# Gathered rows of a product-key expert layer: their use ranked four gathers later with five places, and twelve prompt products ranked ahead of the last picks

## The chip, the cores and the metric

The kernel runs on one core of one Trainium2 chip. The metric is device time in microseconds of one execution. The engines are named as the profile names them: PE (matrix products), DVE (vector work), ACT (activations and copies), POOL (here it issues the gathers and adds a little), SP (issues the plain loads).

## The reference, cut to what matters

Two layers, each an attention part and then a product-key expert layer. The change lies in the second one. Per token and head the two halves of a query are compared with 128 keys each, the best 16 of each half are combined, and the best 16 of the 256 sums are kept: 128 experts per token, each a row of a table of 16384 rows.

```python
def _peer(h, w_pq, k1, k2, u_tab, v_tab):
    ...
        v1, i1 = lax.top_k(s1, P_TOPK)
        v2, i2 = lax.top_k(s2, P_TOPK)
        cand = (v1[..., :, None] + v2[..., None, :]).reshape(m, P_HEADS, P_TOPK * P_TOPK)
        cid = (i1[..., :, None] * N_KEYS + i2[..., None, :]).reshape(m, P_HEADS, P_TOPK * P_TOPK)
        sc, pick = lax.top_k(cand, P_TOPK)
        eid = jnp.take_along_axis(cid, pick, axis=-1)
        g = jax.nn.softmax(sc, axis=-1)
        u = u_tab[eid]
        a = jax.nn.gelu(jnp.einsum('nhkd,nd->nhk', u, xb).astype(f32), approximate=False)
        coef = (g * a).astype(xb.dtype)
        return jnp.einsum('nhk,nhkd->nd', coef, v_tab[eid])
```

There are 256 prompt tokens (two tiles of 128) and 128 sample tokens (one tile).

## The kernel before, in words

**Two ways to the same sum.** The 256 prompt tokens go through all experts: the tables are streamed once, and a table of gates, zero for experts that a token didn't pick, is multiplied in. The 128 sample tokens fetch only their own rows: expert number s of each of the 128 tokens is one gather of 128 rows of 4 KB, 512 KB in all.

**The picks.** `pick` runs for the sample tile (2) first, then for the prompt tiles 0 and 1: `best` finds the halves' best 16, `scores` the sums, `ids` the kept ones. The last steps of `ids(0)` and `ids(1)` transpose ids and gates on PE into PSUM tiles `pit0` and `pit1` (L760, L761), and DVE casts these into `e_i12` and `e_gp` (L762, L764, L765).

**The prompt's stream.** The 16384 experts are cut into 64 pairs of 128-row blocks. For a pair, `first` loads 1 MB of `peer_u`, forms H with PE, and ACT writes Gelu(H) as `co`. `second` loads 1 MB of `peer_v`, multiplies `co` by the gates `G` on DVE (L943) and adds co · v into four PSUM accumulators `acc`. Most products are made in three passes of split numbers (L159, L160, L161): ACT writes the high part (L153, `u_h`, `v_h`, `ch`), DVE the low one (L156, `u_l`, `v_l`, `cl`). The first 16 pairs' H are plain products (`plain_first`, 32 matmuls each, L881; eviction with Gelu to `e_co`, L883) of `hf`, a sum that POOL makes (L869). In `ahead` ten of them, H0 to H9, are emitted behind the whole of `pick`; the other six between the builds. All go through one PSUM pool, `po_`, which has one bank; `at` is a pool of three.

**The gates.** A gate table for 16 blocks is built in 16 steps of 16 tokens: one-hot rows As (DVE L905, or ACT L900), B (DVE L909, L912), their product on PE (`gp`, L920), and an ACT copy to `G`. The 16 builds of tables 0 and 1 stand ahead of `second(0)`; those of the tables 2 to 7 are spread over pairs 8 to 47. As0 of the first 16 builds takes one of the two places of the `peer_v` loads until these builds are through.

**The sample's rows.** `gather_slots` emits gathers behind each pair by `SLOTS`: three per pair up to pair 16, then 4 1/3. The first 128 rows are of `peer_u`: DVE takes the dot product of each with the token's vector (L850). Then come a Gelu and 128 rows of `peer_v`, which DVE adds to `x_s` (L853). There are `ROWB` = 4 places for rows; a gather (POOL, L845) waits until its place is free. Gather and use are emitted together.

**What sets the order.** A list scheduler takes the order in which instructions are emitted as their rank, and puts them on each engine by its own idea of when they are ready. On the chip each engine then works through its list in order: whatever stands first in it holds up all behind it. SP issues the loads of `peer_u` and `peer_v` in its own order, two places for each.

Of the kernel before, what the change touches and what calls it, by code (L numbers as in the profile page):

```python
# [10 lines left out]
F16 = mybir.dt.float16  # L11
# [3 lines left out]
AF = mybir.ActivationFunctionType  # L15
ALU = mybir.AluOpType
# [9 lines left out]
B = 8  # L26
# [15 lines left out]
TB = 16  # L42


PLAIN = (3, 6, 9, 11, 13, 15)
AHEAD = (10, 16)
BUILDS = (((2, 3), 8, 16), ((4, 5), 16, 32), ((6, 7), 32, 48))
SLOTS = ((0, 0), (16, 48), (64, 256))

# [3 lines left out]

RAW = 2
RAWV = 2
ROWB = 4


ORDER = mybir.DependencyInfo(mybir.DependencyClass.NoSync, mybir.DependencyReason.SCHED_ONLY)
# [17 lines left out]
def tile_stream_encoder(ctx: ExitStack, tc: tile.TileContext, I, O, stop=None):  # L77
    nc = tc.nc
    V, S, G, PE = nc.vector, nc.scalar, nc.gpsimd, nc.tensor
# [13 lines left out]
    def po_(name):  # L93
        return pso.tile([128, 512], F32, name=name, tag="po")
# [530 lines left out]
        return out  # L625


    def pick(l, hT, hS, kp, dst, after):

        L = f"l{l}p"  # L630
        qT = kp.tile([128, 8, T], F32, name=L + "_qT", bufs=1)
# [146 lines left out]
        ids(2)  # L778
        best(1, 0)
        best(1, 1)  # L780
        scores(1)
        ids(0)
        ids(1)
# [8 lines left out]
    def peer(l, rest):  # L792
        L = f"l{l}e"
        with tc.tile_pool(name=L, bufs=1, reuse_waits="tile") as lp:

            rings = [lp.tile([128, 4096], F32, name=f"{L}_co{i}", tag="ring", bufs=2) for i in range(2)]
            hT = [lp.tile([128, KC, TP], F32R, name=f"{L}_h{i}") for i in range(2)]
            xn_s = lp.tile([128, D], F32, name=L + "_xn")
            dst = {
                "g": lp.tile([128, 8, 16], F32, name=L + "_g"),  # L800
                "eid": lp.tile([128, 128], I32, name=L + "_eid"),
                "ni1": lp.tile([128, TP], F32, name=L + "_ni1"),
                "i12": lp.tile([128, 2, TP], F16, name=L + "_i12"),
                "gp": lp.tile([128, 2, TP], F16, name=L + "_gp"),
            }
            ex = Experts(l, hT, xn_s, dst, lp, rings)
            with tc.tile_pool(name=L + "k", bufs=2, reuse_waits="tile") as kp:
                def big(name, *shape):
                    return carve(kp.tile([128, 1024], F32, name=name, tag="big", bufs=3), shape)

                hS = [kp.tile([128, KC, 128], F32R, name=f"{L}_hs{i}", tag="dl", bufs=4) for i in range(2)]
                done = norm(I["norm2"][l], lambda t: hS if t == 2 else [h[:, :, t * 128:t * 128 + 128] for h in hT],
                     big, kp, L + "_n2", (2, 0, 1), xn_s, rest)
                pick(l, hT, hS, kp, dst, done[0])
                if stop == (l, "pick"):
                    return
                ex.ahead()
            with tc.tile_pool(name=L + "g", bufs=2, reuse_waits="tile") as gp:
                ex.run(gp)

    class Experts:
        def __init__(self, l, hT, xn_s, dst, lp, rings):
            self.l, self.L, self.hT, self.xn_s, self.dst, self.lp = l, f"l{l}x", hT, xn_s, dst, lp
            self.act = lp.tile([128, 128], F32, name=self.L + "_act")
            self.tables = [I[n].rearrange("l e d -> (l e) d") for n in ("peer_u", "peer_v")]
            self.places = [carve(r, (8, 512)) for r in rings]
            self.co, self.G, self.slot = {}, {}, 0

        def load(self, n, pb):

# [8 lines left out]
        def gather_slots(self, n):  # L839

            for _ in range(min(n, 256 - self.slot)):
                which, s = divmod(self.slot, 128)
                self.slot += 1
                row = self.lp.tile([128, D], F32, name=f"{self.L}_row{which}_{s}", tag="row", bufs=ROWB)
                G.indirect_dma_start(out=row, out_offset=None, in_=self.tables[which],  # L845
                                     in_offset=bass.IndirectOffsetOnAxis(ap=self.dst["eid"][:, s:s + 1], axis=0),
                                     element_offset=self.l * NE * D)
                act = self.act
                if which == 0:
                    V.scalar_tensor_tensor(row, row, 1.0, self.xn_s, op0=ALU.mult, op1=ALU.mult,  # L850
                                           accum_out=act[:, s:s + 1])
                else:
                    V.scalar_tensor_tensor(x[2], row, act[:, s:s + 1], x[2], op0=ALU.mult, op1=ALU.add)  # L853
                if self.slot == 128:
                    S.activation(act, act, AF.Gelu)
                    V.tensor_tensor(act, act, self.dst["g"].rearrange("p h k -> p (h k)"), ALU.mult)

        def ahead(self):

# [13 lines left out]
        def plain_first(self, pbs):  # L873

            L, hf = self.L, self.hf
            for pb in pbs:
                ps = po_(f"{L}_H{pb}")
                u = carve(self.load("u", pb), (2, KC, 128))
                for i in range(2):
                    for k in range(KC):  # L880
# [4 lines left out]
        def build(self, es, tb):  # L885
# [17 lines left out]
            else:  # L903
# [1 line left out]
                V.tensor_tensor(A, iota_2[:, None].to_broadcast([128, NP, 128, 2]), pairs(dst["i12"][:, 0], 128),  # L905
                                ALU.is_equal)
                first = [A[:, t // 2, :, t % 2] for t in range(TB)]
            Bt = carve(self.gp.tile([128, 2 * 48 * TB], F16, name=f"{L}_B{es[0]}{tb}", tag="B"), (2, NP, n, 2))
            V.tensor_tensor(Bt[:, 1], iota_2[:, None, es[0] * 16:es[0] * 16 + n, :].to_broadcast([128, NP, n, 2]),  # L909
                            pairs(dst["i12"][:, 1], n), ALU.is_equal)  # L910
            for i in range(2):
# [177 lines left out]
```

## Time and profile before

| | |
|---|---|
| median of 3 runs | 2651.66 us (2648.11 to 2671.17) |
| profiled execution | 2656.09 us, span 2654.3 us |
| layer 0, layer 1 | about 0 to 1330, 1330 to 2654 us |
| PE busy | 2465.4 us, 93% |
| DVE busy | 2157.9 us, 81% |
| ACT busy | 1416.3 us, 53% |
| POOL busy | 891.0 us, 34% |
| HBM read | 631.48 MB, 240 GB/s over the span |
| mean granted clock of PE | 0.970 |

The busy shares are averages over stages of different kind. In layer 0 the picks end and the first builds begin at about 530 us, the first product of `second` starts at 601.55 us, the last gate build is done at about 1158 us, the last row is used at about 1290 us and the stream ends at about 1328 us; layer 1 repeats this some 1325 us later.

### The profile page before, as it was taken

What the parts mean: (1) busy time and instruction counts of PE and PEld (TensorE: products, weight loads), DVE (VectorE), ACT (ScalarE), POOL (GpSimd) and SP (SyncE); (2) the same over time, 40 slices, a digit from 0 to 9 for tenths busy, and PEclk for the clock granted to TensorE, in tenths of its full rate; (3) what the DMA queues carried; (4) which work ended last, traced back from release to release, by engine and by line L of the source; (5) the groups of instructions that cost most, each with busy time, mean ns of one, the idle gap of its engine ahead of it and who ended that gap; (6) DMA issues with size and microseconds to landing.
All of it is one profiled execution on the core that took longest, in us unless ns stands there. A gap on an engine that the chain in (4) does not pass through costs nothing.

```text
span 2654.3 us, 45318 instructions
## 1 busy us (share of the span) xinstructions
PE 2465.4 (93%) x17316; PEld 2073.8 (78%) x17316; DVE 2157.9 (81%) x4346; ACT 1416.3 (53%) x2594; POOL 891.0 (34%) x587
## 2 busy tenths in 40 slices
PE   7889998898999999999989999988989999999999
PEld 6757777686688888888877677777766888888887
DVE  5754468998999999998767554699989999999986
ACT  4344334273787787744443442332637786876443
POOL 1100010144444565666210000101444455656661
PEclk9999999899999999999999998998999999999999
DMA  4242531498889899999632344314988999999995
GB/s 173 88 128 85 163 120 55 152 352 309 306 321 338 328 340 327 338 345 351 239 112 92 124 132 131 111 57 162 346 316 302 332 334 333 338 329 333 358 349 198
DMA packets 172011, 640.15 MB, mean 241 GB/s; under 512 B 20880, under 2 KB 37008, under 8 KB 139024
## 3 DMA queue, kind: packets, MB, share of 16 engines
q1 hardware_dynamic: 98064, 368.77, 39.0%
q0 software_dynamic: 73728, 268.47, 27.8%
q8 instruction: 136, 2.23, 0.3%
q14 instruction: 83, 0.68, 0.1%
HBM read 631.48 MB, written 5.70 MB: 240 GB/s over the span
## 4 chain that ended last, share of the span: by engine, by line
PE 31%; issue 23%; DVE 18%; POOL 15%; DMA 11%; ACT 2%; POOLq 0%; SPq 0%; DVEq 0%; ACTq 0%
POOL l0x_row L845 8%; POOL l1x_row L845 7%; DMA l0x_row<-in_peer_v_dram,l0e_eid 6%; DMA l1x_row<-in_peer_v_dram,l1e_eid 4%; DVE x_s L853 1%; PE l_g_ps L159 1%; PE l_g_ps L160 1%; PE l_g_ps L161 1%; PE l_pa_ps L159 1%; PE l_pa_ps L160 1%; PE l_pa_ps L161 1%; PE l1x_acc L161 1%; PE l1x_acc L160 1%; PE l1x_acc L159 1%; PE l_br_ps L161 1%
## 5 line engine op out<-in xcount | busy, mean ns | idle before, releaser
L845 POOL DMA_INDIRECT l0x_row<-in_peer_v_dram,l0e_eid x128 | 237.9, 1858 | 152.8 <-DVE x_s L853 135.2
L845 POOL DMA_INDIRECT l1x_row<-in_peer_v_dram,l1e_eid x128 | 238.5, 1863 | 149.4 <-DVE x_s L853 127.1
L845 POOL DMA_INDIRECT l1x_row<-in_peer_u_dram,l1e_eid x128 | 172.0, 1344 | 266.6 <-DVE l1x_row L850 229.7
L845 POOL DMA_INDIRECT l0x_row<-in_peer_u_dram,l0e_eid x128 | 171.1, 1336 | 268.7 <-DVE l0x_row L850 231.0
L161 PE MATMUL l0x_H<-l0e_h,l0x_u_l 128*128 128x256 f32 x768 | 219.7, 286 | 3.6 <-DVE l0x_u_l L156 3.6
L161 PE MATMUL l1x_H<-l1e_h,l1x_u_l 128*128 128x256 f32 x768 | 218.8, 285 | 3.4 <-DVE l1x_u_l L156 3.4
L159 PE MATMUL l0x_H<-l0e_h,l0x_u_h 128*128 128x256 f32 x768 | 221.9, 289 | 0.0
L159 PE MATMUL l1x_H<-l1e_h,l1x_u_h 128*128 128x256 f32 x768 | 221.0, 288 | 0.0
L160 PE MATMUL l0x_H<-l0e_h,l0x_u_h 128*128 128x256 f32 x768 | 219.2, 285 | 0.0
L160 PE MATMUL l1x_H<-l1e_h,l1x_u_h 128*128 128x256 f32 x768 | 218.2, 284 | 0.0
L160 PE MATMUL l0x_acc<-l0x_v_l,l0x_ch 128*128 128x512 f32 x464 | 186.3, 402 | 13.2 <-DVE l0x_v_l L156 13.2
L160 PE MATMUL l1x_acc<-l1x_v_l,l1x_ch 128*128 128x512 f32 x464 | 185.4, 400 | 13.9 <-DVE l1x_v_l L156 13.8
L159 PE MATMUL l0x_acc<-l0x_v_h,l0x_ch 128*128 128x512 f32 x464 | 186.2, 401 | 8.3 <-ACT l0x_v_h L153 4.3
L159 PE MATMUL l1x_acc<-l1x_v_h,l1x_ch 128*128 128x512 f32 x464 | 185.1, 399 | 7.5 <-ACT l1x_ch L153 4.5
L853 DVE SCALAR_TENSOR_TENSOR x_s<-l0x_row,l0x_act,x_s 128x1024 f32<-128x1024 f32 x128 | 166.0, 1297 | 25.1 <-DMA l0x_row<-in_peer_v_dram,l0e_eid 24.4
L161 PE MATMUL l0x_acc<-l0x_v_h,l0x_cl 128*128 128x512 f32 x464 | 183.8, 396 | 0.0
L161 PE MATMUL l1x_acc<-l1x_v_h,l1x_cl 128*128 128x512 f32 x464 | 183.0, 394 | 0.7 <-DVE l1x_cl L156 0.7
L853 DVE SCALAR_TENSOR_TENSOR x_s<-l1x_row,l1x_act,x_s 128x1024 f32<-128x1024 f32 x128 | 164.2, 1282 | 23.8 <-DMA l1x_row<-in_peer_v_dram,l1e_eid 23.0
L850 DVE SCALAR_TENSOR_TENSOR l0x_row<-l0x_row,l0e_xn 128x1024 f32<-128x1024 f32 x128 | 155.9, 1227 | 32.4 <-DMA l0x_row<-in_peer_u_dram,l0e_eid 31.9
L850 DVE SCALAR_TENSOR_TENSOR l1x_row<-l1x_row,l1e_xn 128x1024 f32<-128x1024 f32 x128 | 155.5, 1225 | 31.0 <-DMA l1x_row<-in_peer_u_dram,l1e_eid 30.9
L153 ACT ACTIVATE l0x_v_h<-l0x_v 128x1024 fp32r<-128x1024 f32 x116 | 121.3, 1051 | 98.4 <-DMA l0x_v<-in_peer_vt_dram 51.2
L153 ACT ACTIVATE l1x_v_h<-l1x_v 128x1024 fp32r<-128x1024 f32 x116 | 121.4, 1051 | 96.6 <-DMA l1x_v<-in_peer_vt_dram 47.2
(530 smaller groups left out, 7334.4 us busy)
## 6 DMA issues: line engine op xcount, KB each, us to landing
l0x_u_raw<-in_peer_ut_dram SPq DMA_DIRECT2D x64, 1024.0 KB, 7.1
l0x_v<-in_peer_vt_dram SPq DMA_DIRECT2D x64, 1024.0 KB, 7.5
l1x_u_raw<-in_peer_ut_dram SPq DMA_DIRECT2D x64, 1024.0 KB, 7.3
l1x_v<-in_peer_vt_dram SPq DMA_DIRECT2D x64, 1024.0 KB, 7.6
l_g_raw<-in_w_in_dram SPq DMA_DIRECT2D x16, 1024.0 KB, 4.9
l_pa_raw<-in_w_in_dram SPq DMA_DIRECT2D x8, 1024.0 KB, 5.0
l_kbT<-in_cache_b_kT_dram SPq DMA_DIRECT2D x16, 512.0 KB, 4.0
l_cvb<-in_cache_b_vt_dram SPq DMA_DIRECT2D x16, 512.0 KB, 4.6
```

Source lines behind the costliest of these rows:

```text
L153: op = S.activation(hi, src, AF.Copy)
L159: PE.matmul(out, lh, rh, start=start, stop=False)
L160: PE.matmul(out, lh, rl, start=False, stop=False)
L161: PE.matmul(out, ll, rh, start=False, stop=stop)
L845: G.indirect_dma_start(out=row, out_offset=None, in_=self.tables[which], in_offset=bass.IndirectOffsetOnAxis(ap=self.dst["eid"][:, s:s + 1 ...
L850: V.scalar_tensor_tensor(row, row, 1.0, self.xn_s, op0=ALU.mult, op1=ALU.mult, accum_out=act[:, s:s + 1])
L853: V.scalar_tensor_tensor(x[2], row, act[:, s:s + 1], x[2], op0=ALU.mult, op1=ALU.add)
```

## The change

It has four parts. `ROWB` goes from 4 to 5. The use of a row is emitted when four more gathers have been emitted (`ROWLAG` = 4, `use_row`), so that its rank is that much lower; the last ones are flushed with the 256th gather. `ahead` is handed to `pick` as `meanwhile` and emitted between `best(1, 1)` and `scores(1)`, `ids(0)`, `ids(1)`, with twelve plain products in place of ten, and the plain products go in turn to `po_` and `at`. The tile for B is cut from 48 to 32 columns per token, which are all that a build uses, and frees the room for the fifth row. Lines behind the edits are shifted by one to seven: L850 is L857, L853 L855, L881 L885, L905 L909, L920 L924.

```diff
-AHEAD = (10, 16)
+AHEAD = (12, 16)
...
-ROWB = 4
+ROWB = 5
+ROWLAG = 4
...
         best(1, 1)
+        meanwhile()
         scores(1)
         ids(0)
         ids(1)
...
-                pick(l, hT, hS, kp, dst, done[0])
-                if stop == (l, "pick"):
-                    return
-                ex.ahead()
+                pick(l, hT, hS, kp, dst, done[0], ex.ahead)
...
-                act = self.act
-                if which == 0:
-                    V.scalar_tensor_tensor(row, row, 1.0, self.xn_s, op0=ALU.mult, op1=ALU.mult,
-                                           accum_out=act[:, s:s + 1])
-                else:
-                    V.scalar_tensor_tensor(x[2], row, act[:, s:s + 1], x[2], op0=ALU.mult, op1=ALU.add)
-                if self.slot == 128:
-                    S.activation(act, act, AF.Gelu)
-                    V.tensor_tensor(act, act, self.dst["g"].rearrange("p h k -> p (h k)"), ALU.mult)
+                self.rows.append((which, s, row))
+                while len(self.rows) > (ROWLAG if self.slot < 256 else 0):
+                    self.use_row(*self.rows.pop(0))
+
+        def use_row(self, which, s, row):
+
+            act = self.act
+            if which == 1:
+                V.scalar_tensor_tensor(x[2], row, act[:, s:s + 1], x[2], op0=ALU.mult, op1=ALU.add)
+                return
+            V.scalar_tensor_tensor(row, row, 1.0, self.xn_s, op0=ALU.mult, op1=ALU.mult, accum_out=act[:, s:s + 1])
+            if s == 127:
+                S.activation(act, act, AF.Gelu)
+                V.tensor_tensor(act, act, self.dst["g"].rearrange("p h k -> p (h k)"), ALU.mult)
...
-                ps = po_(f"{L}_H{pb}")
+                ps = (po_, at)[pb % 2](f"{L}_H{pb}")
...
-            Bt = carve(self.gp.tile([128, 2 * 48 * TB], F16, name=f"{L}_B{es[0]}{tb}", tag="B"), (2, NP, n, 2))
+            Bt = carve(self.gp.tile([128, 2 * 32 * TB], F16, name=f"{L}_B{es[0]}{tb}", tag="B"), (2, NP, n, 2))
```

The lists of POOL are the same before and after; on SP the loads of `v0` and `v1` stand one or two `peer_u` loads later. The lists of DVE and PE differ in both layers alike. On DVE of layer 0, where the picks end, the list before was this (`row_2` is a use of gathered row 2, `p_e` a last step of the picks, `e_i` and `e_gp` the casts out of `pit`):

```order
L850 SCALAR_TENSOR_TENSOR l0x_row_2_5233,l0x_act<-l0x_row_2_5233,l0e_xn 128x1024
L735 TENSOR_TENSOR l0p_e_4115<-l0p_we_4110 128x128
L850 SCALAR_TENSOR_TENSOR l0x_row_3_5275,l0x_act<-l0x_row_3_5275,l0e_xn 128x1024
L762 CAST l0e_i_3051<-l0p_pit_4121 128x2x128
L905 TENSOR_TENSOR l0x_As_4344<-iota_91,l0e_i_3051 128x2048
L764 CAST l0e_gp<-l0p_pit_4121 128x128
L909 TENSOR_TENSOR l0x_B_4346<-iota_91,l0e_i_3051 128x512
```

and after it is this:

```order
L857 SCALAR_TENSOR_TENSOR l0x_row_3_5272,l0x_act<-l0x_row_3_5272,l0e_xn 128x1024
L736 TENSOR_TENSOR l0p_e_4366<-l0p_we_4361 128x128
L857 SCALAR_TENSOR_TENSOR l0x_row_4_5274,l0x_act<-l0x_row_4_5274,l0e_xn 128x1024
...
L857 SCALAR_TENSOR_TENSOR l0x_row_14_5393,l0x_act<-l0x_row_14_5393,l0e_xn 128x1024
L763 CAST l0e_i_3051<-l0p_pit_4334 128x2x128
L763 CAST l0e_i_3051<-l0p_pit_4372 128x2x128
L765 CAST l0e_gp<-l0p_pit_4334 128x128
L909 TENSOR_TENSOR l0x_As_4384<-iota_91,l0e_i_3051 128x2048
```

The line of "..." stands for rows 5 to 13, one behind the other. Before, four row uses stood ahead of the first one-hot rows; after, fifteen do, and the casts that the builds begin with stand behind them.

On PE of layer 0, in the same place, the list before was this (H6 to H8 are plain products, `pit` the transposes that the casts read, `gp00` the first build):

```order
L881 MATMUL l0x_H6_4260<-l0x_hf_4137,l0x_u6_raw_4261 128x256 x8
L761 MATMUL l0p_pit0_4083<-cst_70,l0p_g0_3841 128x128
L881 MATMUL l0x_H7_4280<-l0x_hf_4137,l0x_u7_raw_4281 128x256 x12
...
L881 MATMUL l0x_H8_4300<-l0x_hf_4137,l0x_u8_raw_4301 128x256 x7
...
L761 MATMUL l0p_pit1_4121<-cst_70,l0p_g1_4046 128x128
L881 MATMUL l0x_H8_4300<-l0x_hf_4137,l0x_u8_raw_4301 128x256 x9
...
L920 MATMUL l0x_gp00_4352<-l0x_B00_4346,l0x_As0_4344 128x32
```

and after it is this:

```order
L885 MATMUL l0x_H6_4116<-l0x_hf_3993,l0x_u6_raw_4117 128x256 x16
...
L885 MATMUL l0x_H11_4216<-l0x_hf_3993,l0x_u11_raw_4217 128x256 x16
L761 MATMUL l0p_pit0_4334<-cst_70,l0p_fi0_4330 128x128 x2
L762 MATMUL l0p_pit0_4334<-cst_70,l0p_g0_3841 128x128
L761 MATMUL l0p_pit1_4372<-cst_70,l0p_fi1_4368 128x128 x2
L762 MATMUL l0p_pit1_4372<-cst_70,l0p_g1_4297 128x128
L885 MATMUL l0x_H12_4563<-l0x_hf_3993,l0x_u12_raw_4564 128x256 x8
...
L924 MATMUL l0x_gp00_4392<-l0x_B00_4386,l0x_As0_4384 128x32
```

H6 to H11 now stand in one piece ahead of the transposes of both tiles, and four products, H12 to H15, are left for the stretch of the builds, where seven were.

Farther on the row uses stand 9 to 12 rows further in DVE's list than they did. At the split of `v` of pair 20 it was this before (`row0_93` is the 94th row of `peer_u`):

```order
L850 SCALAR_TENSOR_TENSOR l0x_row0_91_8431,l0x_act_3053<-l0x_row0_91_8431,l0e_xn_3047 128x1024
L850 SCALAR_TENSOR_TENSOR l0x_row0_92_8434,l0x_act_3053<-l0x_row0_92_8434,l0e_xn_3047 128x1024
L850 SCALAR_TENSOR_TENSOR l0x_row0_93_8437,l0x_act_3053<-l0x_row0_93_8437,l0e_xn_3047 128x1024
L156 TENSOR_TENSOR l0x_v200_l_7362<-l0x_v20_7359,l0x_v200_h_7361 128x1024
L156 TENSOR_TENSOR l0x_v201_l_7378<-l0x_v20_7359,l0x_v201_h_7377 128x1024
```

and after:

```order
L857 SCALAR_TENSOR_TENSOR l0x_row0_102_8756,l0x_act_3053<-l0x_row0_102_8756,l0e_xn_3047 128x1024
L857 SCALAR_TENSOR_TENSOR l0x_row0_103_8759,l0x_act_3053<-l0x_row0_103_8759,l0e_xn_3047 128x1024
L857 SCALAR_TENSOR_TENSOR l0x_row0_104_8918,l0x_act_3053<-l0x_row0_104_8918,l0e_xn_3047 128x1024
L157 TENSOR_TENSOR l0x_v200_l_7358<-l0x_v20_7355,l0x_v200_h_7357 128x1024
L157 TENSOR_TENSOR l0x_v201_l_7374<-l0x_v20_7355,l0x_v201_h_7373 128x1024
```

So the uses, emitted four gathers later, are placed earlier against the stream: row 104 instead of row 93 stands just ahead of this split. Ahead of the first `cl` (pair 0) it is row 37 instead of 28.

## Rows read from the trace of the kernel before

**Rows 1.** Windows of layer 0 (start:end, length, busy per engine, clock, DMA share, GB/s).

```profile
530.00:601.00 71.00, 66.67 (x749) 57.91 (x748) 66.87 (x123) 50.98 (x128) 32.12 (x26) 1.00 0.94 355
601.00:753.00 152.00, 136.79 (x1005) 99.27 (x1004) 130.09 (x210) 79.77 (x171) 66.07 (x49) 0.93 0.84 307
753.00:1140.00 387.00, 380.47 (x3229) 342.06 (x3228) 370.23 (x462) 298.46 (x575) 215.57 (x124) 1.00 0.91 333
1140.00:1300.00 160.00, 150.54 (x944) 133.56 (x943) 144.28 (x134) 66.40 (x79) 91.44 (x53) 0.97 0.93 342
1300.00:1328.00 28.00, 28.00 (x156) 24.49 (x155) 14.85 (x14) 12.83 (x16) 0.96 (x1) 1.00 0.35 119
```

**Rows 2.** Waits of PE and DVE, 601 to 1328 us (us in total, times, longest).

```profile
PE l0x_acc L160 <- DVE l0x_v_l L156: 13.2, 12, 4.3
PE l0x_gp L920 <- DVE l0x_B L912: 6.0, 6, 1.8
PE l0x_acc L159 <- ACT l0x_v_h L153: 4.3, 1, 4.3
PE l0x_acc L159 <- ACT l0x_ch L153: 4.0, 1, 4.0
PE l0x_H L161 <- DVE l0x_u_l L156: 3.6, 5, 1.9
DVE l0x_row L850 <- DMA l0x_row<-in_peer_u_dram,l0e_eid: 28.3, 21, 5.7
DVE x_s L853 <- DMA l0x_row<-in_peer_v_dram,l0e_eid: 24.4, 23, 2.5
```

**Rows 3.** Timeline of POOL: gathers 4, 5 and 7 (start, us; idle time before).

```profile
524.88 0.94 POOL L845 DMA_INDIRECT l0x_row<-in_peer_u_dram,l0e_eid  x1 [42.13 <-DVE l0x_row L850]
526.41 1.88 POOL L845 DMA_INDIRECT l0x_row<-in_peer_u_dram,l0e_eid  x1 [0.60 <-DVE l0p_we L733]
529.88 1.99 POOL L845 DMA_INDIRECT l0x_row<-in_peer_u_dram,l0e_eid  x1 [0.31 <-issue]
```

**Rows 4.** Timeline of DVE where picks end (start, us; idle time before it).

```profile
523.37 1.23 DVE L850 SCALAR_TENSOR_TENSOR l0x_row<-l0x_row,l0e_xn 128x1024 f32<-128x1024 f32 x1
529.50 0.42 DVE L762 CAST l0e_i<-l0p_pit 128x256 f16<-128x256 f32 x1 [0.73 <-PE l0p_pit L761]
535.11 1.23 DVE L850 SCALAR_TENSOR_TENSOR l0x_row<-l0x_row,l0e_xn 128x1024 f32<-128x1024 f32 x1 [0.33 <-DMA l0x_row<-in_peer_u_dram,l0e_eid]
540.04 1.23 DVE L850 SCALAR_TENSOR_TENSOR l0x_row<-l0x_row,l0e_xn 128x1024 f32<-128x1024 f32 x1 [2.42 <-DMA l0x_row<-in_peer_u_dram,l0e_eid]
```

**Rows 5.** Timeline of PE around the plain products.

```profile
449.04 1.99 PE L881 MATMUL l0x_H<-l0x_hf,l0x_u_raw 128*128 128x256 f32 x8 [2.58 <-POOL l0x_hf L869]
495.71 7.17 PE L881 MATMUL l0x_H<-l0x_hf,l0x_u_raw 128*128 128x256 f32 x32 [0.69 <-ACT l0e_co L883]
507.58 6.16 PE L881 MATMUL l0x_H<-l0x_hf,l0x_u_raw 128*128 128x256 f32 x16 [4.69 <-ACT l0e_co L883]
```

**Rows 6.** DVE from 529.5 to 601.5 us, by form (busy, mean ns, idle before).

```profile
L850 DVE SCALAR_TENSOR_TENSOR l0x_row<-l0x_row,l0e_xn 128x1024 f32<-128x1024 f32 x25 | 30.8, 1231 | 3.8 <-DMA l0x_row<-in_peer_u_dram,l0e_eid 3.6
```

**Rows 7.** Timeline of PE: half-speed products behind two waits.

```profile
658.52 0.79 PE L160 MATMUL l0x_acc<-l0x_v_l,l0x_ch 128*128 128x512 f32 x1 [4.35 <-DVE l0x_v_l L156]
659.11 0.63 PE L161 MATMUL l0x_acc<-l0x_v_h,l0x_cl 128*128 128x512 f32 x1
663.54 0.39 PE L161 MATMUL l0x_acc<-l0x_v_h,l0x_cl 128*128 128x512 f32 x1
```

**Rows 8.** Timeline of DVE and ACT before that: the row and the loads awaited.

```profile
656.09 1.23 DVE L850 SCALAR_TENSOR_TENSOR l0x_row<-l0x_row,l0e_xn 128x1024 f32<-128x1024 f32 x1 [5.66 <-DMA l0x_row<-in_peer_u_dram,l0e_eid]
652.27 2.00 ACT L153 ACTIVATE l0x_v_h<-l0x_v 128x1024 fp32r<-128x1024 f32 x2 [10.34 <-DMA l0x_v<-in_peer_vt_dram]
```

**Rows 9.** Waits of PE, 420 to 601 us.

```profile
PE l0x_H L881 <- ACT l0e_co L883: 13.9, 9, 4.7
```

**Rows 10.** Waits of DVE in layer 1, 1927 to 2648 us.

```profile
DVE l1x_row L850 <- DMA l1x_row<-in_peer_u_dram,l1e_eid: 25.8, 20, 4.8
```

More of the change, by code (lines that the diff above doesn't have):

```diff
@@ L625, in transpose_s, with pick @@
         return out
-    def pick(l, hT, hS, kp, dst, after):
+    def pick(l, hT, hS, kp, dst, after, meanwhile):
         L = f"l{l}p"
@@ L826, in __init__ @@
             self.places = [carve(r, (8, 512)) for r in rings]
-            self.co, self.G, self.slot = {}, {}, 0
+            self.co, self.G, self.slot, self.rows = {}, {}, 0, []
         def load(self, n, pb):
```

## The prediction

> **What bounds the kernel now.** I read the windows by stage first, since the change touches two of them. The reader is to see there which engine has the least slack. In the stretch of the first builds, 530 to 601 us, DVE is busy 66.87 of 71 us, PE 66.67, and the DMA engines run at 0.94 [rows 1]. In the stream behind it PE is the bound: 136.79 of 152 us, 380.47 of 387, 150.54 of 160, 28.00 of 28. So from the start of `second` to its end (727 us) PE has only 15.2 + 6.5 + 9.5 = 31 us without work, and half of that lies in the first 152 us. Then I read who ends PE's waits: 13.2 us for DVE's `v_l`, 6.0 for B, 4.3 and 4.0 for ACT, 3.6 for `u_l`, 31.1 in all [rows 2]. DVE in the same time waits 28.3 + 24.4 = 52.7 us for gathered rows [rows 2]. A split that stands behind an awaited row in DVE's list is late by that wait; the clearest place is 656 us, where DVE waits 5.66 us for a row and PE then 4.35 us for `v_l` [rows 7, 8]. Layer 1 shows the same (25.8 us for its `peer_u` rows) [rows 10], so I work out one layer and double it.
>
> **The change part by part.**
>
> *Row uses ahead of the casts.* This part of the order is what I hold to be decisive at the start of the builds. Before, row uses 0 to 3 stand ahead of the cast, their rows were fetched during the picks, and the casts are done at 529.5 us [rows 4]. Now uses 0 to 14 stand ahead of it. Five gathers can be in flight; the fifth goes out during the picks, as the others do. Gather 5 needs the place of row 0, whose use is over about when it is now, so it goes out at some 524 us, where gather 4 goes out before [rows 3]; gathers 6 to 9 follow each of the next uses by 531 us. From issue to use it took 526.41 to 535.11 us (8.7) and 529.88 to 540.04 (10.2) [rows 3, 4]. Gather 10 goes out when row 5 is used (about 534), gather 14 when row 9 is used. Two rounds of 8.7 us behind the use of row 4 at about 532 us and the last uses end at 532 + 17.4 + 1.2 = 551 us; with 10.2 it is 554, and if the last rows share the DMA engines with plain loads that PE takes one each 7.17 us, 556. The quickest two rounds that I allow, 7.6 us, give 549. The uses themselves, 11 by 1.23 us, are work that is taken from later. PE gets to the transposes at 449.0 + 12 x 7.17 = 535 us at the earliest [rows 5], perhaps 540, so the rows end last. The casts come 21.5 us later than at 529.5 (19.5 to 27).
>
> *The stretch of the builds.* From the cast to the first `cl` DVE had 71.1 us, with 25 row uses and 3.8 us of waits for rows [rows 6]. It now has 23 row uses and none of those waits, but both casts: 71.1 - 3.8 - 2 x 1.3 + 1 = 66 us. PE has four plain products there instead of seven, so DVE stays the bound. A row each 2.9 us, with five in flight and about 9 to 11 us from use to use, leaves the rows in time. `second` starts at 551 + 66 = 617 to 618 us instead of 601.5: **17 us lost** (14 to 22).
>
> *Plain products earlier, in two pools.* PE's waits for the eviction of `e_co`, 13.9 us and up to 4.69 us each, go [rows 5, 9]. They lie where DVE works without pause on the picks, and the builds wait for DVE: nothing is won. If the cover were gone, these 13.9 us would be the price; of a cost of the second pool I see no row; a product that waits there for a bank would do so in the same cover.
>
> *Five places and later use in the stream.* A place goes round in: use, POOL's issue of 0.94 to 1.99 us, 8 to 10 us of transfer, the next use. That is about 11 us. Behind 601 us some 227 rows are used until about 1290, one each 3.0 us on the mean, and rather 2.85 us where there are 4 1/3 per pair instead of three: four places give 11.4 us, just at the edge, which is why DVE waits often and little (24.4 us in 23 waits [rows 2]); five give 14.2 us. So most of the 52.7 us of DVE's waits go. What PE gets of it is bounded: from below by 0 (its waits then come from the `v` loads: at 652.27 us ACT had waited 10.34 us for one [rows 8]), from above by its idle time less what rows don't cause. From 601 to 753 us DVE itself has 130 us of work, and the DMA share of 0.84 would be 0.95 at 134 us, so at most 18 us, with the half-speed products behind the waits included (0.43 instead of 0.23 us from start to start [rows 7]). From 753 to 1140 at most 6.5; from 1140 to 1300 at most 9, without the 4.0 us for `ch`, which is the last build's. Behind it row uses stand about 11 rows further in the list; these 11 x 1.3 us of DVE work and 5.5 MB of transfers were done while it waited for the casts. At the end, where PE is busy 28.00 of 28 us, some 3 us may come from a tail that isn't held by rows. Together **0 to 37 us; I take 25**, two thirds, because the rows are named as what holds the splits, and since PE is at 98% in the longest stretch already.
>
> *B's smaller tile, the SP order.* The same instructions on the same elements: 0. `v0` and `v1` behind one or two more `u` loads are needed only at 617 us: 0.
>
> Sum per layer: +17 - 25 = -8 us, twice -16. The profiled execution took 2656.09 us, so 2640; the median of the runs lies 4.4 us below that execution. **2636 us** as a median.
>
> **The rivals.**
>
> *All row waits go.* The gain is the bound of 37 us, the lost start 17 to 18: -19 per layer, 2651.7 - 38 = **2614**. For it: five places against a cycle just at four's edge. Against it: PE's other sources of waits, and DMA at 0.91 to 0.93.
>
> *The lost start isn't won back (slower).* The mechanism: until As0 gives its place back, `v` loads have one place; then the stream's first 50 us hang on `v` loads, for one of which ACT waited 10.34 us [rows 8]. With five rows in flight these loads share the DMA engines with one gather more, so the `v_h` splits get later, not earlier, and the row waits only change into waits for `v`. With 17 us lost and 0 to 3 won, it is +15 per layer: 2651.7 + 31 = **2683**. It decides when the stream's gain is under some 4 us per layer. Against it: the rows use 11 gathers less of the transfers behind 601 us.
>
> *Only the transposes count.* If the rows land during PE's products, as would be with 4 us per round, the casts run at 540 us: some 6 us are lost after the row uses done early, 25 won, 2651.7 - 38 = **2614** again. Against it are all transfers of [rows 3, 4].
>
> *A slow clock in the builds.* PE would have no work for some 16 us between the transposes and the first build. Behind 4.3 us of waiting twice, products started 0.43 us apart instead of 0.23, until 662.5 us [rows 7]. If PE ran at the low level (1.2 GHz) for the whole stretch of builds, its four plain products (4 x 7.17 = 29 us) and its builds (66.67 us less 7.3 plain products, about 14 us [rows 1, 5]) would take up to twice 43 us, well over DVE's 66, though some of it would lie in PE's pauses: some 7 to 10 us per layer on top, which leaves **2654**. For it: builds are short, and DVE feeds PE piecemeal. Against it: in the builds of before, of the same kind, the granted clock was 1.00 [rows 1]. The Trainium skill, "TensorE: Matmul & The Clock Gate", section "What's actually happening", says that throttled is the default state and that activity releases it, which speaks for this rival; the row at full clock shows release with plain products among the builds, and no row here shows what four instead of seven of them do.
>
> *A rule weighed.* Gathers took POOL 0.94 us at 524.88 and 1.88 and 1.99 us at 526.41 and 529.88, where DVE was at work on picks and tables [rows 3]. The Trainium skill, "SBUF — State Buffer", section "Who interferes with whom", says that POOL's making of descriptors can be shut out by DVE's two-port operations; the trace fits that. While DVE only waits for rows 5 to 14 each gather would then take 0.94 us, and the builds would start 2 us earlier than 551 us. By the rows alone it is 551, which I keep.
>
> **How the numbers follow.** Chances: forecast 0.42 (own range 2618 to 2655, from a gain of 17 to 33 and a start of 14 to 22), all row waits go 0.22, slower 0.20, slow clock 0.08, transposes only 0.08. About 1% (26.5 us) is what a measurement of this kernel can tell: under 2625 is faster, over 2678 slower. Of the forecast a fifth lies under 2625, of the second and the last case most: 0.08 + 0.20 + 0.07 = 0.35. Of the slower case most lies over 2678, with a little of the clock: 0.17. The rest, 0.48, is within 1%. The range leaves out the best tail of the second case and the worst of the third: 2600 to 2688.
>
> **What would show it.** In the profile after: DVE waits for DMA at rows 5 to 14 ahead of the casts, some 15 us, and the first build at 551 us; PE's waits for `e_co` gone; first product of `second` at 617 us; DVE's row waits behind it under 15 us per layer; the 152 us behind the start down to some 137; PE's waits for `v_l` down from 13.2 to under 4 us. The prediction fails if row waits persist at five places (then transfers get longer, not rarer), if `v` loads take the waits over, or if the casts come near 540 us.

## The result and the profile after

Over 15 runs of each, the median went from 2661.06 to 2641.51 us; the ratio is 0.9935 with the interval 0.9919 to 0.9952, some 17 us. The two profiled executions differ by 12.2 us (2656.09 and 2643.86). The page's first lines for the changed kernel:

```profile
span 2642.1 us, 45319 instructions
PE 2447.8 (93%) x17316; PEld 2072.3 (78%) x17316; DVE 2157.1 (82%) x4346; ACT 1421.1 (54%) x2594; POOL 902.9 (34%) x587
```

The instructions are the same to a handful; PE is busy 17.6 us less. First to where the picks end, in DVE's timeline of layer 0 after (start, duration, and in brackets the idle time before and what ended it):

```profile
528.58 1.21 DVE L857 SCALAR_TENSOR_TENSOR l0x_row<-l0x_row,l0e_xn 128x1024 f32<-128x1024 f32 x1
538.48 1.23 DVE L857 SCALAR_TENSOR_TENSOR l0x_row<-l0x_row,l0e_xn 128x1024 f32<-128x1024 f32 x1 [6.00 <-DMA l0x_row<-in_peer_u_dram,l0e_eid]
546.44 1.23 DVE L857 SCALAR_TENSOR_TENSOR l0x_row<-l0x_row,l0e_xn 128x1024 f32<-128x1024 f32 x1 [2.55 <-DMA l0x_row<-in_peer_u_dram,l0e_eid]
552.48 1.22 DVE L857 SCALAR_TENSOR_TENSOR l0x_row<-l0x_row,l0e_xn 128x1024 f32<-128x1024 f32 x1
553.63 0.75 DVE L763 CAST l0e_i<-l0p_pit 128x256 f16<-128x256 f32 x2
```

Against [rows 4] the casts are 24.1 us late. The first line is the use of row 4, the last use is that of row 14, and between them DVE waits 11.4 us in all for gathers (6.00, 2.55 and three shorter waits). PE's timeline over the same stretch and the builds:

```profile
508.40 27.89 PE L885 MATMUL l0x_H<-l0x_hf,l0x_u_raw 128*128 128x256 f32 x128 [0.30 <-ACT l0e_co L887]
536.68 0.27 PE L762 MATMUL l0p_pit<-cst,l0p_g 128*128 128x128 f32 x1
557.13 0.21 PE L924 MATMUL l0x_gp<-l0x_B,l0x_As 128*128 128x32 f16 x1 [14.68 <-DVE l0x_B L916]
623.35 7.63 PE L885 MATMUL l0x_H<-l0x_hf,l0x_u_raw 128*128 128x256 f32 x28
630.64 0.58 PE L160 MATMUL l0x_acc<-l0x_v_h,l0x_ch 128*128 128x512 f32 x1
```

The four products in 27.89 us have no wait for `e_co` left among them, where [rows 9] had 13.9 us. The transposes are done at 537 us; then PE waits for DVE. The first product of `second` comes at 630.64 us instead of 601.55, and in layer 1 at 1945.37 instead of 1927.36, which is 27.6 us later counted from the layer's first norm. PE's and DVE's waits in the builds, 553.6 to 627 us (us in total, times, longest):

```profile
PE l0x_gp L924 <- DVE l0x_B L916: 21.5, 7, 14.7
PE l0x_gp L924 <- ACT l0x_As L904: 17.9, 3, 7.9
DVE l0x_B L913 <- PE l0x_gp L924: 4.1, 2, 2.4
DVE l0x_As L909 <- PE l0x_gp L924: 2.8, 5, 1.3
```

Of the 21.5 us 14.7 are the wait shown above, most of which lies ahead of the casts. In the kernel before, from 529.5 to 600.6 us, PE waited 3.3 us for B and not for As:

```profile
PE l0x_gp L920 <- DVE l0x_B L912: 3.3, 4, 2.1
```

Now it waits for ACT's As too, and DVE waits 6.9 us for PE's gate products. Then the stream. Windows cut at the same work tell more than windows at the same time: from the first product of `second` to the eviction of H16, to that of H31, to that of H63. First the kernel before (start:end, length, busy time of PE, PEld, DVE, ACT, POOL with instructions, PE clock, DMA share, GB/s):

```profile
601.55:719.57 118.02, 105.88 (x739) 74.21 (x738) 101.32 (x164) 62.49 (x136) 49.09 (x38) 0.94 0.84 305
719.57:915.99 196.42, 189.84 (x1614) 168.01 (x1613) 184.46 (x271) 150.04 (x297) 90.14 (x65) 0.97 0.90 330
915.99:1314.23 398.24, 385.75 (x2914) 345.30 (x2913) 365.70 (x378) 238.53 (x402) 234.68 (x125) 0.99 0.91 333
```

and the changed kernel:

```profile
630.64:742.68 112.04, 105.42 (x740) 73.87 (x739) 102.07 (x164) 62.39 (x137) 55.35 (x40) 0.97 0.85 320
742.68:927.43 184.75, 184.75 (x1613) 164.65 (x1613) 182.15 (x259) 150.47 (x296) 100.97 (x65) 1.00 0.94 349
927.43:1304.36 376.93, 376.62 (x2914) 341.91 (x2913) 352.63 (x367) 240.86 (x401) 214.73 (x112) 1.00 0.89 335
```

The stream takes 673.7 us instead of 712.7. The reader should see that two things went: in the two long windows PE's idle time (19.1 us, now 0.3), and 14.2 us of its busy time for the same matmuls, with the clock at 1.00 in place of 0.97 and 0.99. The low level (0.50) accounts for a part of these 14.2 us only. In the two windows of the kernel before it was granted in these four stretches:

```profile
741.23:748.06 6.83, 6.02 (x79) 5.94 (x76) 6.83 (x13) 3.93 (x13) 3.35 (x3) 0.50 0.73 283
901.66:905.07 3.41, 3.41 (x9) 2.65 (x8) 3.34 (x6) 3.41 (x9) 0.45 (x1) 0.50 0.86 312
1154.25:1161.07 6.82, 6.32 (x14) 4.64 (x15) 6.82 (x9) 4.03 (x6) 2.93 (x2) 0.50 0.91 311
1236.17:1239.58 3.41, 3.41 (x18) 3.41 (x17) 3.41 (x4) 1.60 (x3) 1.90 (x2) 0.50 0.86 296
```

PE was busy for 19.2 us of them; at twice the clock that work would take no less than half of that, so the clock makes at most 9.6 us (an estimate from these rows). Where the other 4.6 us come from wasn't taken apart. The waits behind the start, 627 to 1322 us:

```profile
PE l0x_acc L160 <- ACT l0x_v_h L154: 3.0, 1, 3.0
PE l0x_gp L924 <- DVE l0x_B L916: 2.8, 5, 0.9
PE l0x_acc L161 <- DVE l0x_v_l L157: 0.7, 1, 0.7
DVE l0x_row L857 <- DMA l0x_row<-in_peer_u_dram,l0e_eid: 10.0, 11, 2.4
DVE x_s L855 <- DMA l0x_row<-in_peer_v_dram,l0e_eid: 1.7, 4, 0.8
```

They answer to [rows 2]: DVE's 52.7 us for rows are 11.7, PE's 13.2 for `v_l` are 0.7. Layer 0 of the profiled execution gains 39.0 us in the stream and loses 29.1 at its start; the next layer's first transposes start at 1326.48 instead of 1336.10 us. Layer 1 gains less, and the rest of this text reads layer 0 unless it says otherwise: its stream, from the first product of `second` to the eviction of H63, takes 676.28 us instead of 706.52, so 30.2 us are won against the 27.6 lost at the start. First before, then after:

```profile
1927.36:2633.88 706.52, 676.88 (x5263) 583.94 (x5262) 649.37 (x811) 451.34 (x831) 370.70 (x223) 0.99 0.89 328
1945.37:2621.65 676.28, 667.41 (x5263) 580.53 (x5262) 635.43 (x789) 454.27 (x831) 364.57 (x213) 0.99 0.90 333
```

The two layers' balances, 9.9 and 2.6 us, are the 12.2 us of the profiled executions but for 0.3.

### The profile page after: what moved, and what is told of

Read it like the earlier page. It is cut to its first block, busy times and chain, and to the rows that moved or that the text cites. A ratio compares the mean times of both kernels' runs of the same rounds, so it can differ in the third digit from the quotient of the medians.

```text
span 2642.1 us, 45319 instructions
## 1 busy us (share of the span) xinstructions
PE 2447.8 (93%) x17316; PEld 2072.3 (78%) x17316; DVE 2157.1 (82%) x4346; ACT 1421.1 (54%) x2594; POOL 902.9 (34%) x587
## 4 chain that ended last, share of the span: by engine, by line
PE 67%; DVE 17%; issue 8%; POOL 3%; DMA 3%; ACT 2%; SPq 0%; POOLq 0%; ACTq 0%; DVEq 0%
PE l0x_H L160 4%; PE l1x_H L160 4%; PE l0x_H L162 3%; PE l1x_H L162 3%; PE l1x_H L161 3%; PE l0x_H L161 3%; PE l1x_acc L160 3%; PE l1x_acc L161 3%; PE l0x_acc L162 3%; PE l0x_acc L160 3%; PE l1x_acc L162 3%; PE l0x_acc L161 3%; POOL l0x_row L844 2%; POOL l1x_row L844 2%; PE l_g_ps L160 1%
## 5 line engine op out<-in xcount | busy, mean ns | idle before, releaser
L857 DVE SCALAR_TENSOR_TENSOR l1x_row<-l1x_row,l1e_xn 128x1024 f32<-128x1024 f32 x128 | 154.3, 1221 | 25.5 <-DMA l1x_row<-in_peer_u_dram,l1e_eid 25.1
L857 DVE SCALAR_TENSOR_TENSOR l0x_row<-l0x_row,l0e_xn 128x1024 f32<-128x1024 f32 x128 | 154.8, 1223 | 21.9 <-DMA l0x_row<-in_peer_u_dram,l0e_eid 21.5
L855 DVE SCALAR_TENSOR_TENSOR x_s<-l0x_row,l0x_act,x_s 128x1024 f32<-128x1024 f32 x128 | 165.4, 1292 | 3.7 <-DMA l0x_row<-in_peer_v_dram,l0e_eid 1.7
L855 DVE SCALAR_TENSOR_TENSOR x_s<-l1x_row,l1x_act,x_s 128x1024 f32<-128x1024 f32 x128 | 163.6, 1278 | 3.4 <-DMA l1x_row<-in_peer_v_dram,l1e_eid 2.6
```

## The experiments

Two theories: A, the fifth place gains and the new order costs; B, the eleven row uses done while DVE waits for the tables are the gain. All ratios are against the kernel before. In the table are, for layer 0 in us, the last cast of the ids (`e_i`), the start of `second`, the stretch between (builds) and from the start to the eviction of H63 (stream).

| run | casts | start | builds | stream | ratio (95%) |
|---|---|---|---|---|---|
| before | 529.5 | 601.6 | 72.1 | 712.7 | 1 |
| the change | 553.6 | 630.6 | 77.0 | 673.7 | 0.9935 (0.9919 to 0.9952) |
| e1_five_places | 531.2 | 603.8 | 72.7 | 672.4 | 0.9731 (0.9709 to 0.9752) |
| e2_order_only | 551.8 | 631.5 | 79.7 | 711.5 | 1.0235 (1.0209 to 1.0261) |
| e3_casts_first | 536.5 | 613.6 | 77.1 | 675.3 | 0.9818 (0.9791 to 0.9845) |
| e4_ten_ahead | 527.1 | 613.4 | 86.3 | 672.5 | 0.9818 (0.9796 to 0.9841) |
| e5_one_pool | 538.4 | 615.4 | 77.0 | 676.8 | 0.9823 (0.9800 to 0.9845) |
| e6_place_alone | 532.2 | 605.9 | 73.6 | 675.8 | 0.9727 (0.9704 to 0.9750) |
| e7_no_lag | 553.8 | 631.5 | 77.7 | 674.1 | 0.9932 (0.9912 to 0.9953) |
| e8_three_places | 535.9 | 614.6 | 78.7 | 771.8 | 1.0545 (1.0512 to 1.0579) |
| e9_late12 | 531.8 | 603.1 | 71.3 | 674.5 | 0.9702 (0.9674 to 0.9731) |
| e10_late5 | 538.3 | 609.3 | 71.0 | 675.9 | 0.9800 (0.9772 to 0.9828) |
| e11_fill | 553.6 | 649.0 | 95.4 | 681.0 | 1.0088 (1.0054 to 1.0123) |
| e12_dve_rows | 538.4 | 596.2 | 57.8 | 671.1 | 0.9701 (0.9675 to 0.9726) |

**Place and order apart.** e1 is the change with the old order of emission (this diff), e2 the change with the old places (the next):

```diff
-AHEAD = (12, 16)
+AHEAD = (10, 16)
...
-        meanwhile()
         scores(1)
         ids(0)
         ids(1)
+        meanwhile()
...
-                ps = (po_, at)[pb % 2](f"{L}_H{pb}")
+                ps = po_(f"{L}_H{pb}")
```

```diff
-ROWB = 5
-ROWLAG = 4
+ROWB = 4
+ROWLAG = 0
```

> Five places and the late use alone: the first products are ranked behind the whole of the picks again, ten of them, in one PSUM pool, so the lists of DVE and PE stand as before the change (four row uses ahead of the first one-hot rows). Theory A (the changed kernel's gain comes from the fifth place, and its order costs it 29 us of start per layer, 630.6 against 601.5 us): second starts near 600 us, DVE's row waits fall from 52.7 us to under 15, and the layer gains 25 to 35 us, so 0.974 to 0.981 of before. Theory B (the gain comes from the eleven row uses that are done while DVE waits for the picks' tables, the place alone does little): 0.995 to 1.000 of before, with PE's waits of 31 us mostly still there, put down to v loads.

> The order alone: twelve products ranked ahead of the last picks in two pools, with four places and each row's use emitted with its gather; 14 row uses stand ahead of the casts. Theory A: the casts come at 555 us or later (rounds of four in place of five), second starts near 630, the row waits stay near 40 us, and each layer loses 10 to 25 us: 1.008 to 1.019 of before. Theory B: as the changed kernel or a little less, 0.990 to 0.998.

Theory A holds: -2.7% and +2.4%, both a little beyond the ranges given for it. The windows of e1:

```profile
603.84:715.02 111.18, 104.18 (x739) 73.02 (x738) 102.70 (x165) 62.64 (x137) 51.33 (x38) 0.98 0.87 324
715.02:899.85 184.83, 184.83 (x1614) 164.74 (x1613) 183.49 (x272) 150.74 (x297) 96.13 (x65) 1.00 0.95 353
899.85:1276.26 376.41, 376.41 (x2914) 342.13 (x2913) 363.36 (x376) 240.84 (x401) 228.60 (x124) 1.00 0.93 349
```

Its stream is that of the changed kernel, though its row uses stand 9 to 12 rows less far. And e2, with uses as far on as in the changed kernel, streams as slowly as the kernel before:

```profile
631.49:1342.95 711.46, 681.02 (x5263) 586.64 (x5262) 641.49 (x791) 451.39 (x832) 360.01 (x218) 0.98 0.88 320
```

So the lead of the rows is worth nothing that shows (e1, with less of it, is 1.3 us shorter than the changed kernel, e2, with more, 1.2 us shorter than the kernel before), which fells B. In e2 the casts came at 551.8 us, not at 555 or later, and the loss was more than the 1.9% that I allowed: I had given the lead some worth.

**The place by itself, the late use by itself, fewer places.** e6 and e8 are e1 with `ROWLAG = 0`, so the kernel before with the smaller B and another count of places (the diff, against the kernel before, is e6's; e8 has `ROWB = 3`); e7 is the change with `ROWLAG = 0` alone.

```diff
-ROWB = 4
+ROWB = 5
...
-            Bt = carve(self.gp.tile([128, 2 * 48 * TB], F16, name=f"{L}_B{es[0]}{tb}", tag="B"), (2, NP, n, 2))
+            Bt = carve(self.gp.tile([128, 2 * 32 * TB], F16, name=f"{L}_B{es[0]}{tb}", tag="B"), (2, NP, n, 2))
```

> The kernel before with the fifth place (and B's smaller tile) and nothing else: each use is emitted with its gather, ten products behind the picks, one pool. The row uses stand as in the run with five places and the late use. If the place does it: 0.971 to 0.976 of before, the same as that run (0.9731) within 0.002. If the late rank has a part in it: over 0.978.

> The changed kernel with each row's use emitted with its gather. The lists of PE are those of the changed kernel and those of DVE differ in a few neighbouring rows, so the late rank has nothing to act on: 0.991 to 0.996 of before, as the changed kernel. If late use matters by itself: over 1.00.

> The kernel before with three places (and B's smaller tile). If the round of a place bounds the rows (about 10.5 to 11 us from use to use, so 3.5 to 3.7 us per row with three): 227 rows behind the start take 800 to 840 us instead of 690, the stream hangs on them, and each layer takes 70 to 130 us more: 1.05 to 1.10 of before. If the rows' waits come from the DMA engines' share rather than from the places, three in flight land faster and it is 1.00 to 1.03.

e6 equals e1 and e7 equals the change: the later rank does nothing measurable. The stream of e6:

```profile
605.87:1281.71 675.84, 667.42 (x5263) 580.91 (x5262) 648.77 (x811) 451.93 (x832) 381.63 (x225) 0.99 0.93 344
```

With three places DVE's waits from 614 to 1400 us double:

```profile
DVE x_s L855 <- DMA l0x_row<-in_peer_v_dram,l0e_eid: 59.8, 51, 3.7
DVE l0x_row L857 <- DMA l0x_row<-in_peer_u_dram,l0e_eid: 49.4, 34, 5.2
```

The stream is 59 us longer than with four and `second` starts 13 us later; by the medians (2801.28 and 2660.40 us) a layer takes 70 us more, at the lower end of the 70 to 130 expected. From four to five places it is 37 to 40 us. So the round of a place holds up the stream with three and with four. No run has a sixth place.

**What of the order costs.** To the change, e3 adds an edge in the scheduler's graph (the diff; `cast` is the last DVE step out of `pit`); e4 is the change with e1's line on `AHEAD` alone, e5 with its line on `po_` alone.

```diff
-            V.scalar_tensor_tensor(row, row, 1.0, self.xn_s, op0=ALU.mult, op1=ALU.mult, accum_out=act[:, s:s + 1])
+            op = V.scalar_tensor_tensor(row, row, 1.0, self.xn_s, op0=ALU.mult, op1=ALU.mult, accum_out=act[:, s:s + 1])
+            if s >= 4:
+                tc.add_manual_dep(op.ins, self.dst["cast"], ORDER)
```

> The changed kernel with one scheduling edge: the uses of rows 4 and later stand behind the casts out of pit, so four row uses stand ahead of the casts instead of fifteen. Theory A: the casts come at 537 us, when PE has made the transposes, instead of 553.6; the builds' stretch stays at 70 us or more since PE has only four plain products in it; second starts near 614 us, and each layer gains 8 to 16 us over the changed kernel: 0.981 to 0.988 of before. Theory B: the eleven uses come back into the stream at 1.3 us each and their transfers too, so nothing is won: 0.992 to 0.996 of before.

> The changed kernel with ten plain products ranked ahead instead of twelve: five row uses stand ahead of the casts, PE makes the transposes after H9, and six plain products lie among the builds. Theory A: the casts come at about 530 us, the granted clock in the builds is 0.95 or more (0.74, 0.80 and 0.55 in the three parts of that stretch of the changed kernel), second starts near 600 us, and the time is that of the run with five places alone: 0.974 to 0.981 of before. Theory B: 0.990 to 1.000 of before.

> The changed kernel with all plain products in the one-bank pool again; twelve are still ranked ahead of the last picks. In its lists the casts stand ahead of all row uses, eight uses stand ahead of the first one-hot B, and PE has pit's transposes between H6 and H8 and six whole products among the builds. If the order of the changed kernel (twelve products in one piece, 15 uses ahead of the casts) costs the start, and the second pool is what lets the list become so: the first B comes at 541 us or earlier, the clock in the builds is 0.9 or more, second starts at 604 to 612 us, 0.973 to 0.980 of before. If the rank of the twelve alone costs it, whatever the pools: 0.988 to 0.996.

e3 is as expected. Its first cast (behind PE's transposes) and its first product of `second`:

```profile
536.52 0.76 DVE L763 CAST l0e_i<-l0p_pit 128x256 f16<-128x256 f32 x2 [8.00 <-PE l0p_pit L762]
613.64 0.58 PE L160 MATMUL l0x_acc<-l0x_v_h,l0x_ch 128*128 128x512 f32 x1
```

Without the eleven uses the casts come 17.1 us sooner, and all of it stays (start 17.0 us sooner). That part of the lost start is shown; 7 us more are PE's, whose transposes stand behind twelve products, and the last 5 the longer builds. e4 and e5 missed: their casts are early (527.1, 538.4), but their builds take 86.3 and 77.0 us. In e4 PE waited 7.2 us for one `u` load there and the clock was 0.80; e5 had the clock at 0.95. Why e4 takes so long wasn't taken apart further.

**What bounds the builds.** e9 is e6 with an edge like that of e3, which holds the uses from row 12 on behind the last B of the first builds (`if s >= 12`, `self.last_b`); e10 is e7 with that edge from row 5 on. e11 is the change with added work, six PE products behind each first build whose result nothing reads (first diff); e12 is e10 with the second.

```diff
+            ps = at(f"{self.L}_fill{tb}")
+            for k in range(6):
+                op = PE.matmul(ps[:, 0:TP], ident, self.hf[:, k, :], start=True, stop=True)
+                tc.add_manual_dep(op.ins, self.last_gp, ORDER)
```

```diff
-ACT_ROWS = {0: (1, 4, 7, 10, 13), ...
+ACT_ROWS = {0: (), ...
```

> The kernel with the fifth place alone, and a scheduling edge: the uses of rows 12 and later stand behind the last one-hot B of the first builds, so 12 uses instead of 28 stand ahead of it. If DVE's row uses in the builds set the start: 16 uses by 1.31 us leave DVE 51 us there, PE's 66 us decide, second starts at 597 to 600 us instead of 604 to 606; but the stream gets 21 us of DVE work and 8 MB more, with DVE at 657 and DMA at 0.94 there. I expect the start's gain to be given back: 0.968 to 0.977 of before. If the DMA engines bound the stream, it is slower than the place alone: over 0.977.

> The changed kernel with each use emitted with its gather, and the edge from row 5 on: five uses stand ahead of the casts and none in the builds. The casts come at 537 us with PE's transposes; DVE has some 40 us of work in the builds, PE 43 us at full clock, ACT 49 us, so second starts at 586 to 595 us instead of 630.6. The stream gets 23 uses (30 us of DVE) and 12 MB more than in the run with the place alone and becomes bound by DVE or DMA, 690 to 700 us instead of 686: 0.962 to 0.974 of before. If the low clock in the builds grows with the missing products (0.76 in the run with the casts first), PE needs 60 us there, start near 600, and it is 0.972 to 0.980.

> The changed kernel with six more PE products behind each of the 16 first builds, into a PSUM tile that nothing reads; twelve more row uses come to stand ahead of the first cl by it (50 instead of 38). If the low clock (0.71 over the builds of the changed kernel) is what makes DVE and ACT wait for PE's gate products there: the clock is over 0.95 in the builds, DVE's 6.9 us of waits for gp fall under 2 us, H15's 28 products take 6.3 us instead of 7.63; the twelve uses take 15 us more, which come back later only in part: 0.988 to 1.000 of before. If the clock has no part in it, the waits for gp stay at 6 us or more.

> The run with no row uses in the builds (five ahead of the casts), and DVE makes the one-hot rows As of all 16 first builds; ACT made them for five of the 16 until now. With no row uses and DVE busy only 45 of 71 us that stretch was as long as before, and PE waited 16.0 us there for ACT's As, behind ACT's wait for a plain product. If this ring of ACT's As and PE's products sets the stretch: DVE has 51 us of work, PE 48, ACT 15, the stretch falls from 71 to 53 to 60 us, second starts at 591 to 598 us, and the layer gains 11 to 18 us on that run: 0.966 to 0.972 of before. If the ring is that of PE's gate products and DVE's two places for As (14.5 us of waits there), the stretch stays at 66 to 73 us and the time at 0.977 to 0.983.

e9 and e10 refute my view that DVE's row uses set the length of the builds: in e9 16 fewer shorten it by 2.3 us (73.6 to 71.3), and in layer 1 not at all (73.5 and 73.7), and in e10, with none, it is still 71.0 (77.7 in e7), DVE being busy 45.46 of 71. Both starts missed their ranges (603.1 for 597 to 600, 609.3 for 586 to 595). In e10 the uses held back also outlast the stream: its last row is used at 1304.8 us, behind the eviction of H63 at 1285.2. The windows over the builds of e10:

```profile
538.00:609.00 71.00, 47.73 (x643) 41.22 (x642) 45.46 (x85) 49.79 (x129) 3.66 (x3) 0.78 0.39 139
```

and of e12:

```profile
538.00:598.00 60.00, 48.99 (x654) 42.01 (x653) 52.03 (x93) 19.97 (x48) 5.73 (x4) 0.86 0.48 175
```

ACT's timeline in e10 shows the ring: a Gelu of a plain product stands ahead of the next build's As, and waits for PE,

```profile
578.73 0.60 ACT L889 ACTIVATE l0e_co<-l0x_H 128x512 f32<-128x512 f32 x1 [7.26 <-PE l0x_H L887]
581.15 3.90 ACT L904 ACTIVATE l0x_As<-iota,l0e_ni 128x128 f16<-128x128 f16 x13
585.09 1.91 ACT L906 ACTIVATE l0x_As<-l0x_As 128x2048 f16<-128x2048 f16 x1
```

and then PE waits for that As:

```profile
569.97 8.72 PE L887 MATMUL l0x_H<-l0x_hf,l0x_u_raw 128*128 128x256 f32 x32
587.05 1.89 PE L928 MATMUL l0x_gp<-l0x_B,l0x_As 128*128 128x32 f16 x64 [6.77 <-ACT l0x_As L906]
```

With As made by DVE (e12) the stretch falls by 13.2 us and the ratio from 0.9800 to 0.9701. So it is shown, for a kernel without row uses in the builds, that ACT's As set their length. An As takes ACT over 5.8 us (3.90 and 1.91 above) and DVE 1.2 us; how much is that and how much the wait of the Gelu ahead of it was not separated. In e11 the clock over the builds was 0.92 instead of 0.71 (over 0.95 was expected), DVE's waits for gate products fell from 6.9 to 2.3 us, PE's for As from 17.9 to 1.3, and H15's 28 products took 6.2 us instead of 7.63. But the stretch grew to 95.4 us, since twelve more row uses came into it (DVE busy 84.8 us), and the ratio, 1.0088, lies above the 0.988 to 1.000 expected: the low clock and the waits go together, yet e11 doesn't tell what of the 77 us is the clock's. Across the runs the clock doesn't sort the lengths: 0.95 with 77.0 us (e5), 0.78 with 71.0 (e10), 0.86 with 57.8 (e12).

e9, e12, e6 and e1 are all faster than both kernels; their intervals overlap, and the simplest of them is e6, the kernel before with a fifth place.

## Why the prediction was right, step by step

The forecast was -16 us; -17 were measured by the ratio (-12 in the profiled executions). The signs and places were right; two terms were mis-sized, in layer 0 by 12 and 14 us and in layer 1 by 11 and 5, against each other, so the sum owes its closeness in part to luck.

- **Row uses ahead of the casts**: 551 us expected (549 to 556), 553.63 measured. Right, and e3 shows that this and nothing else holds the casts from 537 us on. The two rounds were not alike, though: from issue to use rows 5 and 6 took 5.3 to 5.6 us, rows 7 to 11 10.2 to 15.1 and rows 12 to 14 8.3 to 10.0, where the sum has 8.7, so that it is luck how near the end came.
- **The builds' stretch, "DVE stays the bound"**: this is the step that was wrong, 77.0 us where 66 were forecast. DVE's own work there was as worked out: from the cast to the first `cl` (626.52 us) 72.9 us, less 6.9 of waits, is 66.0. But the waits for PE's gate products were not in the sum, nor H15, which stands last in PE's list ahead of `second` and takes 7.63 us for 28 of its 32 products, so that PE starts 4.1 us behind the first `cl`. 2.6 + 6.9 + 4.1 = 13.6 us is the whole error (630.64 against 617). The loss was 29.1 us, not 17 (14 to 22).
- **Plain products earlier, in two pools, at nothing**: right as to PE's waits (13.9 us went to 0.3, and nothing came of it). But I didn't see that four products instead of seven in the builds have a price: the slow-clock rival came true in its mechanism, 0.71 over 553.6 to 631 us where [rows 1] had 1.00. How much of the 11 us it made stays open.
- **Five places in the stream, 25 us of at most 37**: mis-sized; 39.0 measured in layer 0 (40.3 in e1) and 30.2 in layer 1. For layer 0 the bound itself was too low (and was added up too high: 160 less 150.54 less the 4.0 for `ch` is 5.5, not 9, so its terms give 33). I took PE's busy time as fixed, 98% in the long stretch [rows 1]; but of the 39.0 us only 24 were idle time, and 15 were busy time for the same matmuls: 14.2 of them lie in the two long windows, and the low clock makes at most 9.6 of these.
- **"These 11 x 1.3 us of DVE work" as a part of the gain**: wrong; the uses' lead made no difference (e1 against the change, e2 against before).
- **B's tile, the SP order, at nothing**: not run by themselves. The tile stands in e2 too, whose stream is as long as before; nothing speaks against 0.
- **The rivals**: "all row waits go" was right for the stream of layer 0, which even beat it, and 7 us too high for layer 1; "the lost start isn't won back" was nearer than I thought, since the start lost 29 us (27.6 in layer 1): with the stream's gain at the forecast's 25 each layer would have lost 3 to 4 us. "Only the transposes count" is out by DVE's 11.4 us of waits for rows ahead of the casts.

The rule weighed needs a closer reading. In the changed kernel gathers that began while DVE waited for rows took POOL 0.94 us (all 33 of the execution that began with DVE idle took 0.93 or 0.94), and two that began inside a row use (from 539.84 and 549.93 us) took 1.89 and 1.79 us, until 0.8 us behind the end of that use:

```profile
539.98 1.89 POOL L844 DMA_INDIRECT l0x_row<-in_peer_u_dram,l0e_eid  x1 [5.46 <-DVE l0x_row L857]
547.95 0.94 POOL L844 DMA_INDIRECT l0x_row<-in_peer_u_dram,l0e_eid  x1 [2.84 <-DVE l0x_row L857]
550.17 1.79 POOL L844 DMA_INDIRECT l0x_row<-in_peer_u_dram,l0e_eid  x1 [1.29 <-DVE l0x_row L857]
```

A row use reads two tiles in SBUF, and a gather reads its ids there. The Trainium skill, "SBUF — State Buffer", section "Who interferes with whom", says that a DVE instruction with two SBUF inputs contends with a POOL instruction that reads SBUF; the trace fits that. It is this, and not a two-port mode of DVE, that the rows bear on: the long gathers of [rows 3] began inside a row use (526.27 us) and a one-hot As (529.84 us). Where both begin within 0.05 us of each other it can go either way: the short gather, at 524.88 us, began 0.03 us behind a row use, and the one of 1.99 us 0.04 behind that As; what decides there stays open. The start that the rule would have given, 2 us ahead of 551, did not come: most gathers of rows 5 to 14 took 0.93 to 1.14 us, and the casts were 2.6 us later: the landings decided, since all of DVE's 11.4 us of waits there end on a DMA.

## What to carry to other kernels

Where a wait is followed by slow products, cost it twice: its idle time, and the longer busy time of the work behind it; compare windows cut at the same work, not at the same time, to see both. Check a combined change by its parts: here one number (a fifth place) held -2.7% and the rest gave most of it back. Before calling one engine the bound of a stretch, list what the engines in the ring wait for from each other; taking DVE's row uses out of the builds shortened them by 6.7 us (e10 against e7), and moving ACT's As to DVE by another 13.2.

## What the runs showed of the hardware that was not expected

PE's granted clock fell to the low level in the stream behind waits of 1.8 to 4.4 us: in the four stretches shown above, and at the waits of 4.30 and 4.35 us that end at 653.38 and 658.52 us ([rows 7] has the second). In the four stretches this cost at most 9.6 us of PE's 575.6 busy us in the two long windows. In the changed kernel, where PE gets four products among the builds instead of seven, the clock over that stretch was 0.71 instead of 1.00, and 0.92 with added PE work there (e11).

A gather's issue on POOL took 0.94 us with DVE idle, and up to 1.99 us where a DVE instruction with two inputs was running ([rows 3], and the lines at 539.98 and 550.17 us).
